# A two-layer trunk on one core: the front made token tile by token tile, the next quarter's rows in fewer steps, and one store on another queue

## The chip, the cores and the metric

The kernel runs on one core of a Trainium2 chip. The core has five engines, each with its own queue of instructions, which it takes in order: TensorE (PE in the profile; matmuls, its weight loads are PEld), VectorE (DVE), ScalarE (ACT), GpSimd (POOL) and SyncE (SP). SP computes nothing here; it issues DMA transfers between DRAM and the on-chip memory. The metric is the device time of one execution in microseconds (us).

## The reference, cut to what matters

The input is x, 2048 tokens of 1024 channels in float32, and a conditioning vector c of 1024. One layer of gMLP type is followed by one layer of attention type; both work on a normed and modulated x:

```python
def ada_mod(c, w, b, n):
    h = jax.nn.silu(c) @ w + b
    return jnp.split(h[:, None, :], n, axis=-1)

def gmlp_layer(x, c, ada_w, ada_b, norm_g, w_in, sgu_g, w_s, b_s, w_out):
    shift, scale, gate = ada_mod(c, ada_w, ada_b, 3)
    h = rms_norm(x, norm_g) * (1 + scale) + shift
    u, v, z = jnp.split(h @ w_in, 3, axis=-1)
    u = jax.nn.gelu(u)
    v = rms_norm(jax.nn.gelu(v), sgu_g)
    ...
    return x + gate * (y @ w_out)

def dilated_layer(x, c, kv_groups, ada_w, ada_b, norm_g, w_in, q_norm_g, w_out):
    shift, scale, gate = ada_mod(c, ada_w, ada_b, 3)
    h = rms_norm(x, norm_g) * (1 + scale) + shift
    qz = h @ w_in
    ...
    return x + gate * (y @ w_out)
```

Between the two, one set of keys and values for the attention is made from x after the first layer (w_kv). The widths that matter: u, v and z have 2048 columns each; the queries have three groups of 1024 columns and z of the second layer 1024.

## The kernel before

**Tiling.** The 2048 tokens are worked in four quarters Q of 512 tokens, each of four token tiles t of 128. The 1024 channels are eight slices k of 128. Every product of activations and weights is made of three matmuls (mm3, L214): both sides are split into a high part, rounded to the PE's faster float32 form, and the low rest, and high x high, high x low and low x high are added up in PSUM. So each weight tile of 128x512 is loaded into a tile "raw", copied by ACT into its high half (L187) and subtracted by DVE into its low half (L188) before PE can use it. hA (hAh and hAl) is the split, normed and modulated x of a quarter, transposed: channels on partitions, tokens along the row.

**The stages.** `begin` makes hA for the first quarter and the first two of four column blocks (j = 0, 1) of its v. Then for each quarter `layer_A` makes the rest of v, the mixing, u, z and the output product, adds it to x (the tiles xr, `done`), stores the sum x1d for the last stage, and norms it; `proj_B` makes from it keys and values (kv blocks), and queries and z of the second layer in blocks of 512x512 (q_block(2), kv, q_block(1), q_block(0), z_block). These last blocks (`dense_s`, and `dense_s2` for v of the later quarters) save an eighth of the products by working with sums of blocks: seven products of 24 matmuls each, on operands such as "s2" and weights such as wt, sums of blocks that were made once and stored in DRAM. m in the later quarters holds such sums of parts of hA.

**The front.** `begin` squares the eight slices of x (already transposed by the host) on ACT, adds them up over the channels with matmuls of one column (pssq), takes the power -1/2 on POOL (L816), and broadcasts the result over partitions with a matmul on a diagonal (prb). Meanwhile silu(c) is spread over all partitions (scb), and DVE makes scale and shift of each slice k as dots of scb with rows of the weights a_ada (aw; L152). The first slice of hA is made on DVE and ACT straight from prb (z0); slices 2 to 7 are multiplied with rb, a copy of prb, by POOL (L865). The products run slice by slice: for each k two column blocks j, four tiles t, three matmuls, 24 in all. `busy` puts transposes into PE's queue that compute nothing.

**Fillers.** Side work is written as Python generators. `tick` is called after the matmuls of each slice and lets the generators go on, by a share `rate` of a step each time; `drain` runs what is left to its end. `make_hA` is such a generator: during q_block(1), q_block(0) and z_block of one quarter, with rate 0.9, it prepares hA of the next. It loads x by rows, squares them on ACT, takes the reciprocal norms r on POOL, stores r to DRAM (rd, L710: 128x4 numbers, each a piece of 4 bytes), reads it back spread over all partitions (rb, L175), multiplies the transposed x (xT) with it, and for each k scales (h_a), splits (hAh by ACT, hAl by POOL) and stores h_a to DRAM (hd, L723), from which the parts of m are loaded (L743) for the sums. A `yield` in it is a stop; there are 27.

**What sets the order.** The build puts each engine's instructions into one fixed order, near that in which the code is written. Nearly all DMA transfers are issued by SP, one after the other, so one that waits for its data holds back all behind it. They run on 16 DMA engines, and SP waits, before it issues one, until the one eight places ahead of it has landed. Transfers land in about the order of their issue.

## Time and profile before

| | us |
|---|---|
| three executions | 2979.52, 2973.64, 2977.4 |
| median | 2977.4 |
| the profiled execution | 2983.25 |
| its span (first to last instruction) | 2981.5 |
| PE busy | 2889.6 |
| DVE, ACT, POOL busy | 2140.4, 1659.8, 772.2 |

The mean clock granted to PE is 0.988 of full speed; DMA moves 720.6 MB, 242 GB/s on average. PE is busy in 97% of the span, so the questions are where its holes lie and what ended them. In rows of a timeline the columns are start, duration, engine, line, operation, out<-in, shape and count, and in brackets how long the engine stood idle before it and what released it; numbers of tiles are left out of the names. In rows of SP the duration is that of issuing, not of the transfer.

### The profile page before, as it was taken

To read this page: it belongs to the slowest core of one execution; us is meant where nothing else is said; L and a number is where in the kernel's file an instruction comes from. 1 tells how busy PE (TensorE), PEld (TensorE's weight loads), DVE (VectorE), ACT (ScalarE), POOL (GpSimd) and SP (SyncE) were. 2 spreads that over 40 slices of the span, in tenths; PEclk is the share of its full clock that TensorE was granted. 3 is DMA by queue.
4 is the path that set the end of the run, shared out by engine and by line. 5 is a ranking of instruction groups with operands and counts; after the bars stand their busy time and mean duration, and the time that the engine had idled before them with its cause. 6 is when DMAs were issued, how large, how long until landed. Compare 5 with 4: busy or idle time off the path is not lost.

```text
span 2981.5 us, 45378 instructions
## 1 busy us (share of the span) xinstructions
PE 2889.6 (97%) x14519; PEld 2434.3 (82%) x14519; DVE 2140.4 (72%) x3997; ACT 1659.8 (56%) x3403; POOL 772.2 (26%) x1042
## 2 busy tenths in 40 slices
PE   8999999899999999899999999899999999999999
PEld 7788877787888878778888878778888888888887
DVE  6787467677777886767767876777759676877782
ACT  4433344567676355566655365676646366876541
POOL 2047432230000413510233403401314111122312
PEclk9999999999999999999999999999999999999999
DMA  6899977896789976787545977874335966788753
GB/s 230 276 333 340 308 259 212 254 306 216 252 302 306 347 237 218 244 283 241 179 131 165 343 236 231 260 262 142 107 111 182 361 214 219 246 265 323 241 176 110
DMA packets 389730, 720.60 MB, mean 242 GB/s; under 512 B 45426, under 2 KB 141810, under 8 KB 389492
## 3 DMA queue, kind: packets, MB, share of 16 engines
q1 hardware_dynamic: 389492, 717.71, 72.4%
q8 instruction: 115, 1.88, 0.3%
q14 instruction: 123, 1.01, 0.1%
HBM read 559.60 MB, written 157.96 MB: 241 GB/s over the span
## 4 chain that ended last, share of the span: by engine, by line
PE 63%; DMA 5%; DVE 3%; issue 3%; ACT 2%; POOL 1%; SPq 0%; POOLq 0%; DVEq 0%; ACTq 0%
PE pd_kv L216 6%; PE po L1314 4%; PE pd_z L260 3%; PE pd_z L258 3%; PE pd_z L259 3%; PE pd_u L260 3%; PE pd_u L258 3%; PE pd_u L259 3%; PE pd_o3a L216 1%; PE pd_o1a L216 1%; PE pd_o2a L216 1%; PE pm L900 1%; PE pd_v3b L216 1%; PE pq L1204 1%; PE pf L1498 1%
## 5 line engine op out<-in xcount | busy, mean ns | idle before, releaser
L216 PE MATMUL pd_kv<-w_kv,hkh 128*128 128x512 f32 x672 | 210.0, 393 | 2.8 <-DVE w_kv L188 2.3
L258 PE MATMUL pd_u<-hAh,w_u 128*128 128x512 f32 x512 | 206.4, 403 | 0.0
L258 PE MATMUL pd_z<-hAh,w_z 128*128 128x512 f32 x512 | 204.2, 399 | 0.0
L260 PE MATMUL pd_u<-hAh,w_u 128*128 128x512 f32 x512 | 200.5, 392 | 2.9 <-DVE w_u L188 2.9
L260 PE MATMUL pd_z<-hAh,w_z 128*128 128x512 f32 x512 | 200.0, 391 | 0.0
L259 PE MATMUL pd_u<-hAl,w_u 128*128 128x512 f32 x512 | 199.5, 390 | 0.0
L259 PE MATMUL pd_z<-hAl,w_z 128*128 128x512 f32 x512 | 199.4, 389 | 0.0
L1314 PEld LDWEIGHTS po<-kv,pT 128*128 128x128 f32 x1200 | 148.0, 191 | 11.0 <-ACT pT L1160 2.8
L1314 PE MATMUL po<-kv,pT 128*128 128x128 f32 x1200 | 150.6, 275 | 3.3 <-ACT pT L1160 2.3
L187 ACT ACTIVATE w_u<-raw_u 128x512 fp32r<-128x512 f32 x128 | 79.6, 629 | 132.9 <-DMA raw_u<-in_a_w_in_dram 54.2
L187 ACT ACTIVATE w_z<-raw_z 128x512 fp32r<-128x512 f32 x128 | 78.7, 628 | 129.6 <-PE pd_z L260 64.9
L216 PEld LDWEIGHTS pd_kv<-w_kv,hkh 128*128 128x128 f32 x672 | 125.9, 189 | 30.5 <-DVE w_kv L188 3.9
L1262 POOL TENSOR_TENSOR dg<-pr,ident 128x256 f32<-128x256 f32 x38 | 31.7, 833 | 424.8 <-DMA st_o<-od 226.6
L188 DVE TENSOR_TENSOR w_z<-raw_z,w_z 128x512 fp32r<-128x512 f32 x128 | 102.2, 806 | 53.5 <-ACT w_z L187 53.1
L216 PE MATMUL pd_kv<-w_kv,hkl 128*128 128x512 f32 x336 | 131.1, 391 | 0.0
L1085 POOL TENSOR_SCALAR s_q<-s_q 128x4 f32<-128x4 f32 x96 | 24.8, 258 | 386.7 <-DVE s_q L1084 288.1
L1254 ACT ACTIVATE pr<-pr,stat,rt 128x256 f32<-128x256 f32 (+1 forms) x192 | 104.1, 544 | 34.2 <-DVE stat L1248 19.9
L187 ACT ACTIVATE w_q<-raw_q 128x512 fp32r<-128x512 f32 x144 | 88.9, 627 | 52.7 <-DMA raw_q<-in_b_w_in_dram 17.8
L260 PEld LDWEIGHTS pd_u<-hAh,w_u 128*128 128x128 f32 x512 | 96.1, 188 | 24.6 <-DVE w_u L188 3.7
L188 DVE TENSOR_TENSOR w_q<-raw_q,w_q 128x512 fp32r<-128x512 f32 x144 | 96.7, 694 | 24.4 <-ACT w_q L187 23.4
L260 PEld LDWEIGHTS pd_z<-hAh,w_z 128*128 128x128 f32 x512 | 96.1, 188 | 20.8
L259 PEld LDWEIGHTS pd_z<-hAl,w_z 128*128 128x128 f32 x512 | 96.3, 188 | 18.1
(881 smaller groups left out, 8577.4 us busy)
## 6 DMA issues: line engine op xcount, KB each, us to landing
raw_q<-in_b_w_in_dram SPq DMA_DIRECT2D x144, 256.0 KB, 3.8
w_o<-wtd SPq DMA_DIRECT2D x72, 512.0 KB, 5.3
raw_u<-in_a_w_in_dram SPq DMA_DIRECT2D x128, 256.0 KB, 4.1
raw_z<-in_a_w_in_dram SPq DMA_DIRECT2D x128, 256.0 KB, 3.6
wtd<-cs SPq DMA_DIRECT2D x56, 512.0 KB, 3.9
raw_v<-in_a_w_in_dram SPq DMA_DIRECT2D x104, 256.0 KB, 4.0
qt<-qd SPq DMA_DIRECT2D x96, 260.0 KB, 3.3
od<-ot SPq DMA_DIRECT2D x96, 256.0 KB, 3.3
```

The costliest lines, as they stand in the source:

```text
L187: nc.scalar.activation(hi, src, AF.Copy)
L188: nc.vector.tensor_tensor(lo, src, hi.bitcast(F32), ALU.subtract)
L216: last_mm[0] = nc.tensor.matmul(pt, a, u[:, w, :], start=f, stop=e, skip_group_check=more)
L258: nc.tensor.matmul(pts[i], wh, hh[:, k, :], start=k == 0, stop=False)
L259: nc.tensor.matmul(pts[i], wh, hl[:, k, :], start=False, stop=False)
L260: nc.tensor.matmul(pts[i], wl, hh[:, k, :], start=False, stop=k == KT - 1)
L900: nc.tensor.matmul(pm[:, t * P:(t + 1) * P], m[e // 8][:, t, (e % 8) * P:(e % 8 + 1) * P], wst[:, e // 2, :], start=True, stop=True)
L1204: nc.tensor.transpose(pq[:, h * P:(h + 1) * P], u["qt"][:, h * P:(h + 1) * P], ident)
L1254: nc.scalar.activation(pr[:, i, :], pr[:, i, :], AF.Exp, bias=mneg[:, i:i + 1], scale=u["rt"][:, h:h + 1], accum_out=lsum[:, i:i + 1])
L1262: nc.gpsimd.tensor_tensor(dg, prev, ident.unsqueeze(1).broadcast_to([P, hp, P]), ALU.mult)
L1314: nc.tensor.matmul(po[:, h * P:(h + 1) * P], u["pT"][h // hp][:, h % hp, j, :], u["kv"][:, j, kh, 1, :], start=j == 0, stop=j == nk - 1)
L1498: nc.tensor.matmul(pt, yb[:, 0, k, :], w_[:, 0, :], start=k == 0, stop=False)
```

## The change

**1. The front.** x of the first quarter comes from the host by token tiles (xt0), each one transfer of 128 partitions x 8 slices x 128 tokens (512 KB, in pieces of 512 bytes on chip). Each tile is squared (`square`), normed, broadcast and scaled (`rows`) by itself, POOL multiplying slices 2 to 7 of one tile at a time, and the products of k=0 run tile by tile behind it; from k=1 on they run slice by slice as before, with the two column blocks of a tile next to each other. The ada rows of k=0 are loaded first, then c, then x. Fillers on PE stand between the steps. **2. make_hA**: two tiles are squared in one step, the loads of xT and the store of r share a step, and each k has one stop instead of two: 16 in all. **3.** The store of x1d of the first quarter (where `fast` is false) is issued by ACT instead of SP.

In the hunk of `begin`, "..." stands for the removed lines (L774 to L867 above).

```diff
@@ -695,7 +695,8 @@
         yield
         sq = sp.tile([P, 16], F32, tag="sqa", bufs=1, name=f"sqa{Q}")
         for t in range(TPQ):
-            yield
+            if t == 2:
+                yield
             for h in range(2):
                 j = evt(f"sqj{Q}{t}{h}")
                 nc.scalar.activation(j, xts[t][:, h * 512:(h + 1) * 512], AF.Square,
@@ -705,18 +706,17 @@
         r = rstd_of(sq[:, 8:12], TPQ, D, f"r_a{Q}")
         zs = [xp.tile([P, 2, QT], F32, tag="xin", name=f"xT{Q}_{k2}") for k2 in range(0, KT, 2)]
         for i, z in enumerate(zs):
-            nc.sync.dma_start(z, xt[Q, :, 2 * i:2 * i + 2, :])
-        yield
+            nc.sync.dma_start(z, xt[Q - 1, :, 2 * i:2 * i + 2, :])
         nc.sync.dma_start(rd[Q].rearrange("t p -> p t"), r[:, 0:TPQ])
         yield
         yield
         rb = bcast(rd[Q:Q + 1].rearrange("o t p -> o (t p)"), f"rb{Q}")
         yield
         yield
+        yield
         for k in range(KT):
             z = zs[k // 2][:, k % 2, :]
             nc.vector.tensor_tensor(z, z, rb, ALU.mult)
-            yield
             h = evt(f"h_a{Q}_{k}")
             nc.scalar.activation(h, z, AF.Identity, scale=aff[0][:, k:k + 1], bias=aff[1][:, k:k + 1])
             nc.scalar.activation(hA[0][:, k, :], h, AF.Copy)
@@ -771,107 +771,139 @@
         xT = big.tile([P, KT, QT], F32, tag="big", name="xT0")
         one = rp.tile([P, 512], F32, tag="raw", name="one")[:, 0:P]
         nc.vector.memset(one, 1.0)
...
+        crow = wp.tile([P, D], F32, tag="w", name="crow")[0:1, :]
+        aws, raws, us = {}, {}, {}
+        def load_aw(k, i):
+            if k % 2 == 0 and k not in aws:
+                t = big.tile([P, 2, 2, D], F32, tag="big", name=f"aw{k}")
+                aws[k], aws[k + 1] = t[:, 0], t[:, 1]
+            nc.sync.dma_start(aws[k][:, i, :], a_ada[i * KT + k])
+        def load_w(k):
+            for j in range(2):
+                raws[k, j] = rp.tile([P, 512], F32, tag="raw", name=f"raw_v0{j}_{k}")
+                nc.sync.dma_start(raws[k, j], a_w_in[k * P:(k + 1) * P, AW + j * 512:AW + (j + 1) * 512])
+        def w_high(k, j):
+            us[k, j] = wp.tile([P, 2, 512], F32R, tag="w", name=f"w_v0{j}_{k}")
+            nc.scalar.activation(us[k, j][:, 0, :], raws[k, j], AF.Copy)
+        def w_low(k, j):
+            nc.vector.tensor_tensor(us[k, j][:, 1, :], raws[k, j], us[k, j][:, 0, :].bitcast(F32), ALU.subtract)
+        def load_xt(t):
+            nc.sync.dma_start(xT[:, :, t * P:(t + 1) * P], xt0[t])
+        load_aw(0, 1)
+        nc.sync.dma_start(crow, c)
+        load_aw(0, 0)
+        nc.sync.dma_start(vecs, cols)
+        load_xt(0)
+        load_xt(1)
+        load_w(0)
+        load_xt(2)
+        load_xt(3)
+        def dots(k, i):
+            ks = slice(k, k + 1)
+            ada_dot(aff[1 - i][:, ks], aws[k][:, i, :], aab_c[:, i * KT + k:i * KT + k + 1])
+            if i:
+                nc.vector.scalar_tensor_tensor(aff[0][:, ks], aff[0][:, ks], 1.0, ang_c[:, ks],
+                                               ALU.add, ALU.mult)
+        pq = pst("pq0")
+        prb = pst("prb", "d")
 
         def busy(n):
...
             for _ in range(n):
...
+                nc.tensor.transpose(pq[:, 256:384], ident, ident)
         r = sp.tile([P, 16], F32, tag="sqa", bufs=1, name="sqa0")
...
+        rb, diag, z0, h0 = (evt(f"{n}0") for n in ("rb", "diag", "z", "h"))
+        def square(t):
+            j = wp.tile([P, KT, P], F32, tag="w", name=f"sqT{t}")
+            nc.scalar.activation(j, xT[:, :, t * P:(t + 1) * P], AF.Square)
+            for k in range(KT):
+                nc.tensor.matmul(pq[:, t:t + 1], j[:, k, :], one[:, 0:1], start=k == 0, stop=k == KT - 1)
+            nc.vector.tensor_scalar(r[:, t:t + 1], pq[:, t:t + 1], 1.0 / D, EPS, ALU.mult, ALU.add)
+            nc.gpsimd.tensor_tensor(r[:, t:t + 1], r[:, t:t + 1], mhalf[:, 0:1], ALU.pow)
+        def rows(t):
             sl = slice(t * P, (t + 1) * P)
             nc.scalar.activation(diag[:, sl], ident, AF.Copy, scale=r[:, t:t + 1])
             nc.tensor.matmul(prb[:, sl], one, diag[:, sl], start=True, stop=True)
...
+            nc.vector.tensor_tensor(z0[:, sl], xT[:, 0, sl], prb[:, sl], ALU.mult)
+            nc.scalar.activation(hA[0][:, 0, sl], z0[:, sl], AF.Identity, scale=aff[0][:, 0:1],
+                                 bias=aff[1][:, 0:1])
+            nc.vector.tensor_scalar(h0[:, sl], z0[:, sl], aff[0][:, 0:1], aff[1][:, 0:1], ALU.mult, ALU.add)
+            nc.vector.tensor_tensor(hA[1][:, 0, sl], h0[:, sl], hA[0][:, 0, sl].bitcast(F32), ALU.subtract)
+            nc.scalar.activation(rb[:, sl], prb[:, sl], AF.Copy)
+            nc.gpsimd.tensor_tensor(xT[:, 2:KT, sl], xT[:, 2:KT, sl],
+                                    rb[:, sl].unsqueeze(1).broadcast_to([P, KT - 2, P]), ALU.mult)
+        pts = {}
+        def products(k, t):
+            sl = slice(t * P, (t + 1) * P)
+            for j in range(2):
+                if k == 0:
+                    pts[j, t] = pst(f"pd_v0{j}_{t}", "da"[j])
+                mm3(pts[j, t], hA[0][:, k, sl], hA[1][:, k, sl], (us[k, j]), k == 0, k == KT - 1)
+        busy(4)
+        for n in range(2):
+            pc = pst(f"pc{n}")
+            nc.tensor.matmul(pc, one[0:1, :], crow[:, n * 512:(n + 1) * 512], start=True, stop=True)
+            nc.scalar.activation(scb[:, n * 512:(n + 1) * 512], pc, AF.Silu)
+        busy(30)
+        dots(0, 1)
+        dots(0, 0)
+        square(0)
+        busy(6)
+        square(1)
+        w_high(0, 0)
+        rows(0)
+        w_low(0, 0)
+        w_high(0, 1)
+        w_low(0, 1)
+        busy(4)
+        for t in range(TPQ):
+            products(0, t)
+            if t + 2 < TPQ:
+                square(t + 2)
+            busy(4)
+            if t == 2:
+                for i in (1, 0):
+                    load_aw(1, i)
+                load_w(1)
+                dots(1, 1)
+            if t + 1 < TPQ:
+                rows(t + 1)
+        for k in range(1, KT):
             h = xT[:, k, :]
             if k == 1:
+                dots(1, 0)
                 nc.vector.tensor_tensor(h, h, rb, ALU.mult)
...
+            nc.scalar.activation(h, h, AF.Identity, scale=aff[0][:, k:k + 1], bias=aff[1][:, k:k + 1])
+            split(hA[0][:, k, :], hA[1][:, k, :], h)
+            for j in range(2):
+                w_high(k, j)
+                w_low(k, j)
             if k + 1 < KT:
...
+                for i in (1, 0):
+                    load_aw(k + 1, i)
+                load_w(k + 1)
+                dots(k + 1, 1)
+                dots(k + 1, 0)
+            for t in range(TPQ):
+                products(k, t)
         m, sqv = v_tiles(0)
         for j in range(2):
             ev = v_evac(0, m, sqv, j)
             for t in range(TPQ):
...
+                ev(t, pts[j, t])
         return hA, m, sqv
 
     def layer_A(Q, hA, m, sqv, j0):
@@ -971,7 +1003,7 @@
             if seen[t] == 2:
                 tt = Q * TPQ + t
                 def store():
-                    nc.sync.dma_start(x1d[tt * P:(tt + 1) * P, :], xts[t])
+                    (nc.sync if fast else nc.scalar).dma_start(x1d[tt * P:(tt + 1) * P, :], xts[t])
                 if fast:
                     stores.append([0, store])
                 else:
@@ -1567,7 +1599,8 @@
                                      "a_sgu_g", "k_norm_g", "b_q_norm_g")]
     return {
         "x": x,
-        "xt": np.ascontiguousarray(x[0].reshape(NQ, QT, KT, P).transpose(0, 3, 2, 1)),
+        "xt0": np.ascontiguousarray(x[0, :QT].reshape(TPQ, P, KT, P).transpose(0, 3, 2, 1)),
+        "xt": np.ascontiguousarray(x[0, QT:].reshape(NQ - 1, QT, KT, P).transpose(0, 3, 2, 1)),
         "c": np.asarray(i["c"]),
         "cols": np.ascontiguousarray(np.concatenate(cols, axis=1)),
         "a_ada": _tiles(np.asarray(i["a_ada_w"])[0]),
```

How this moves instructions, at three places. First DVE in the front; affa 180 and 181 are scale and shift, sqa takes the sums of squares, w_v is a weight's low half. Before, from the last sum of squares on:

```order
L815 TENSOR_SCALAR sqa_290<-pssq_213 128x1
L152 ISA aw_315,affa_180<-aw_315,scb,vecs 128x1024
L152 ISA affa_180 128x1
L829 SCALAR_TENSOR_TENSOR affa_180<-affa_180,vecs 128x1
L842 TENSOR_TENSOR z_331<-xT_188,prb 128x512
L152 ISA aw_315,affa_181<-aw_315,scb,vecs 128x1024
L152 ISA affa_181 128x1
L856 TENSOR_TENSOR xT_188<-xT_188,rb_338 128x512
L843 TENSOR_SCALAR xT_188<-z_331,affa_180,affa_181 128x512
L846 TENSOR_TENSOR w_v_0_322<-raw_v_0_321,w_v_0_322 128x512
L847 TENSOR_TENSOR hAl_187<-xT_188,hAh_186 128x512
L848 TENSOR_TENSOR w_v_0_326<-raw_v_0_325,w_v_0_326 128x512
```

Now:

```order
L152 ISA aw_192,affa_180<-aw_192,scb,vecs 128x1024
L152 ISA affa_180 128x1
L152 ISA aw_192,affa_181<-aw_192,scb,vecs 128x1024
L152 ISA affa_181 128x1
L812 SCALAR_TENSOR_TENSOR affa_180<-affa_180,vecs 128x1
L793 TENSOR_TENSOR w_v_0_285<-raw_v_0_199,w_v_0_285 128x512
L830 TENSOR_SCALAR sqa_207<-pq_205 128x1
L793 TENSOR_TENSOR w_v_0_296<-raw_v_0_201,w_v_0_296 128x512
L152 ISA aw_192,affa_180<-aw_192,scb,vecs 128x1024
L152 ISA affa_180 128x1
L830 TENSOR_SCALAR sqa_207<-pq_205 128x1
L837 TENSOR_TENSOR z_210<-xT_188,prb 128x128
```

The dots of k=0 stand ahead of the first norm now, and operations on a single tile (128x128) alternate with weight halves and dots of k=1, so each of these can hold the tile behind it.

Second, SP in q_block(1) and the product after it, for the first quarter; wt_1, wt_0 and wt_3 name the weights of three products. Before:

```order
L195 DMA raw_q00t_0_5105<-wt_1_108 128x512
L195 DMA raw_q00t_1_5110<-wt_1_108 128x512
L708 DMA xT_6_5014<-in_xt_dram 128x1024
L710 DMA rd<-r_a_5008 128x4x1
L195 DMA raw_q00t_2_5115<-wt_1_108 128x512
L195 DMA raw_q00t_3_5120<-wt_1_108 128x512
L195 DMA raw_q_0_5151<-in_b_w_in_dram 128x512
L175 DMA rb_5184<-rd 128x512
L195 DMA raw_q_1_5156<-in_b_w_in_dram 128x512
```

Now:

```order
L1123 DMA qd_94<-st_q02w_4348 128x520
L1123 DMA qd_94<-st_q02w_4349 128x520
L709 DMA xT_2_4848<-in_xt_dram 128x1024
L709 DMA xT_4_4849<-in_xt_dram 128x1024
L709 DMA xT_6_4850<-in_xt_dram 128x1024
L710 DMA rd<-r_a_4844 128x4x1
L195 DMA raw_q01t_0_4867<-wt_0_111 128x512
L195 DMA raw_q01t_1_4872<-wt_0_111 128x512
L195 DMA raw_q01t_2_4877<-wt_0_111 128x512
L195 DMA raw_q01t_3_4882<-wt_0_111 128x512
L1123 DMA qd_94<-st_q02u_4067 128x520
L1123 DMA qd_94<-st_q02u_4068 128x520
```

The store of r (rd) stood between the weight tiles of wt_1; now it stands, right behind the loads of xT, ahead of those of wt_0, which are used four products earlier.

Third, SP at the end of the z block; raw_v and raw_v14t are weights of the next quarter's v. Before:

```order
L723 DMA hd<-h_a_5_5851 128x2x256
L723 DMA hd<-h_a_6_5857 128x2x256
L723 DMA hd<-h_a_7_5863 128x2x256
L195 DMA raw_v_0_6039<-in_a_w_in_dram 128x512
L195 DMA raw_v_1_6044<-in_a_w_in_dram 128x512
L195 DMA raw_v_2_6049<-in_a_w_in_dram 128x512
L743 DMA m_1_5872<-hd 128x1024 x2
L195 DMA raw_v_3_6054<-in_a_w_in_dram 128x512
L195 DMA raw_v14t_0_6089<-wt_1_124 128x512
```

Now the last two stores of h_a:

```order
L195 DMA raw_z0bt_0_5665<-wt_2_121 128x512
L195 DMA raw_z0bt_1_5670<-wt_2_121 128x512
L723 DMA hd<-h_a_6_5533 128x2x256
L723 DMA hd<-h_a_7_5587 128x2x256
L1207 DMA kv_2_7181<-kvd 128x512
```

and, some twenty rows further on, the loads of m:

```order
L195 DMA raw_z0b_2_5833<-in_b_w_in_dram 128x512
L195 DMA raw_z0b_3_5838<-in_b_w_in_dram 128x512
L743 DMA m_1_5878<-hd 128x1024 x4
L1131 DMA zd<-zb_2_5762 128x512
L1131 DMA zd<-zb_3_5765 128x512
L195 DMA raw_v_0_5891<-in_a_w_in_dram 128x512
```

The stores of h_a stood among the weights of v, with two of the loads of m behind them; now the last of them is among the weights of the z block (raw_z0bt), and all four loads of m stand ahead of the first raw_v.

More of the change, by code (lines that the diff above doesn't have):

```diff
@@ L791, in units @@
-        def units(k):
-            us[k] = [wunits(a_w_in, k, AW + j * 512, f"v0{j}_{k}_", 1)[0] for j in range(2)]
+        crow = wp.tile([P, D], F32, tag="w", name="crow")[0:1, :]
[9 more added lines that the diff above has]
+                nc.sync.dma_start(raws[k, j], a_w_in[k * P:(k + 1) * P, AW + j * 512:AW + (j + 1) * 512])
@@ L796, in busy @@
             for _ in range(n):
-                nc.tensor.transpose(pw[:, 0:P], ident, ident)
-        for n in range(2):
-            pc = pst(f"pc{n}")
-            nc.tensor.matmul(pc, one[0:1, :], crow[n], start=True, stop=True)
-            nc.scalar.activation(scb[:, n * 512:(n + 1) * 512], pc, AF.Silu)
-        pqs = [pst(f"pssq{t}", "d") for t in range(TPQ)]
-        sqs = [evt(f"sqT{k}") for k in range(4)] + [rp.tile([P, 512], F32, tag="raw", name=f"sqT{k}")
-                                                    for k in range(4, KT)]
@@ L806, in begin @@
-        for k in range(KT):
-            nc.scalar.activation(sqs[k], xT[:, k, :], AF.Square)
-            for t in range(TPQ):
-                nc.tensor.matmul(pqs[t][:, 0:1], sqs[k][:, t * P:(t + 1) * P], one[:, 0:1],
-                                 start=k == 0, stop=k == KT - 1)
-            if k + 1 < KT:
-                busy(3)
-        r = sp.tile([P, 16], F32, tag="sqa", bufs=1, name="sqa0")
-        for t in range(TPQ):
-            nc.vector.tensor_scalar(r[:, t:t + 1], pqs[t][:, 0:1], 1.0 / D, EPS, ALU.mult, ALU.add)
```

64 lines of the change are left out of this document (1 added, 63 removed).

## Prediction

> **What bounds the kernel now.** I read the busy table first, then what TensorE (PE) waited for, then the timelines around each long wait. A row of the waits reads: who waited, for which engine's tile; us in all, times, longest.
>
> ```profile
> PE 2889.6 (97%) x14519; PEld 2434.3 (82%) x14519; DVE 2140.4 (72%) x3997; ACT 1659.8 (56%) x3403; POOL 772.2 (26%) x1042
> ...
> PE pd_q00b L216 <- DVE st_q01u L511: 8.9, 1, 8.9
> PE pd_q20b L216 <- DVE st_q21u L511: 7.9, 1, 7.9
> PE pd_q10b L216 <- DVE st_q11u L511: 7.4, 1, 7.4
> PE pt_b L637 <- DVE xr L984: 6.8, 2, 6.4
> PE pd_v1a L216 <- ACT w_v14t L187: 4.3, 1, 4.3
> PE pd_v2b L216 <- ACT w_v L187: 3.3, 1, 3.3
> PE pd_v3b L216 <- ACT w_v L187: 3.1, 1, 3.1
> ...
> PE pd_v2b L216 <- ACT hAh L722: 2.1, 1, 2.1
> ...
> PE pd_v3b L216 <- ACT hAh L722: 1.3, 1, 1.3
> ```
>
> PE is the bound: 2889.6 of 2981.5 us, so only 92 us of holes are there to be won, and the change adds or removes almost no matmul time. The rows name three families, each of which comes once for each of the later quarters: the q products (24.2 us), the start of the v products of the next quarter (14.1 us), and one wait of 6.4 at the end of the first quarter. A fourth place is the front, before PE streams at all:
>
> ```profile
> 33.00 0.73 PE L216 MATMUL pd_v<-w_v,hAh 128*128 128x512 f32 x2 [1.28 <-ACT hAh L844]
> ...
> 46.17 2.11 PE L216 MATMUL pd_v<-w_v,hAh 128*128 128x512 f32 x8 [0.59 <-ACT hAh L187]
> ```
>
> The first real product runs at 33.0 us, and k=1 starts at 46.17, after which no row of the timeline has a wait until the last product of the front. So the front is worth exactly what moves the start of k=1: seven steps of 24 matmuls follow, whatever came before.
>
> **The front.** Removed: a norm over all 512 tokens before anything is multiplied. In its place come 4 tiles of 128 tokens, each with its own square, power, broadcast and scaling, and fillers on PE which cost nothing as long as PE has only holes there. What sets the first step is the first tile's x and the silu behind it:
>
> ```profile
> 4.29 0.63 ACT L807 ACTIVATE sqT<-xT 128x512 f32<-128x512 f32 x1 [2.23 <-DMA xT<-in_xt_dram]
> 4.94 1.28 ACT L802 ACT_TABLE_LOAD   x1
> 6.23 1.09 ACT L802 ACTIVATE scb<-pc 128x512 f32<-128x512 f32 x2
> ...
> 11.94 0.63 ACT L807 ACTIVATE sqT<-xT 128x512 f32<-128x512 f32 x1 [0.29 <-DMA xT<-in_xt_dram]
> 24.80 2.06 POOL L816 TENSOR_TENSOR sqa<-sqa,mhalf 128x4 f32<-128x4 f32 x1 [21.27 <-DVE sqa L815]
> 26.89 1.28 ACT L822 ACTIVATE diag<-ident,sqa 128x128 f32<-128x128 f32 x4 [14.32 <-POOL sqa L816]
> ```
>
> Eight slabs of 256 KB came between 4.29 and 11.94, 1.09 us each. The first tile (512 KB) now stands behind two ada pieces of 512 KB: six slabs, so 4.29 + 5 x 1.09 = 9.7 us. ACT then does in order a square of twice the width (1.1, estimated from 0.63), a table load 1.28, a silu 0.55, the second tile's square 1.1, a silu 0.55: 14.3. DVE's order has both dots of k=0 ahead of the first norm (1.28 each), and one weight low half: 17.7. The power takes 2.06: 19.8. From the power to the first broadcast matmul 0.5 us, then quarter-width z and hAh, some 1 us: the first product at about 21.3 instead of 33.0.
>
> But k=1 comes only when DVE is through. By its order, from the first norm to the multiplication for k=1 it does 5 dots, 6 low halves, 12 operations of quarter width and that multiplication. What these take depends on POOL:
>
> ```profile
> 31.29 9.75 POOL L865 TENSOR_TENSOR xT<-xT,rb 128x512 f32<-128x512 f32 x6 [4.43 <-ACT rb L850]
> 34.78 1.74 DVE L846 TENSOR_TENSOR w_v<-raw_v,w_v 128x512 fp32r<-128x512 f32 x1
> 42.05 1.27 DVE L152 CUSTOM_DVE_ANT_0 aw<-aw,scb,vecs 128x1024 f32<-128x1024 f32 x1
> 44.64 0.82 ACT L858 ACTIVATE xT<-xT,affa,affa 128x512 f32<-128x512 f32 x1 [10.65 <-DVE affa L829]
> 47.12 0.69 DVE L188 TENSOR_TENSOR hAl<-xT,hAh 128x512 fp32r<-128x512 f32 x1
> ```
>
> A subtraction of this width took 1.74 while POOL multiplied and 0.69 after: a factor of 2.5. Undisturbed, 5 x 1.28 + 6 x 0.65 + 12 x 0.25 (estimated from 0.69 for four times the width) + 0.69 + 0.5 = 14.5 us, from 17.7 to 32.2. POOL's work is unchanged in elements, four bursts of 9.75/4 = 2.44 us, all now inside this stretch: they cost DVE 9.75 x (1 - 1/2.5) = 5.9: 38.1. ACT's scaling 0.82 and high half 0.63 follow: k=1 at about 39.5, 6.7 us before 46.17. I take **7**. Upper bound: no disturbance, 33.6, a gain of 12.6. Lower: POOL's whole 9.75 added to DVE and 5 us more for dots that wait in DVE's row for the later ada pieces, which no row prices: 48.4, a loss of 2.
>
> The Trainium skill (SBUF — State Buffer, "SBUF: two separate sides") says that DVE and GpSimd hold their shared port pair as an exclusive lock, the later one blocked for the whole instruction. The rows agree so far (1.74 against 9.75/6 = 1.63 for one POOL operation), and by the rule POOL's 9.75 us would be added whole: 3.9 us less gain than I take. The sum goes by the rows' factor.
>
> **Scaled rows in fewer steps.** For each later quarter a filler squares x, writes the reciprocal norms r to DRAM (rd, L710), reads them back as a broadcast (rb) and makes hA. It has 27 stops before and 16 after, and the three product blocks it runs in step it 3 blocks x 7 products x 4 x 0.2857 x 0.9 = about 21.6 times, so now it can end inside them. What the r store does to the queue is the cause of the 8-us stalls:
>
> ```profile
> 560.40 0.33 SPq L708 DMA_DIRECT2D xT<-in_xt_dram  x1
> 565.35 0.37 SPq L710 DMA_DIRECT2D rd<-r_a  x1
> 565.81 0.93 SPq L195 DMA_DIRECT2D raw_q00t<-wt  x2
> 578.33 0.63 ACT L187 ACTIVATE w_q00t<-raw_q00t 128x512 fp32r<-128x512 f32 x1 [13.21 <-DMA raw_q00t<-wt]
> 1868.29 12.01 DMA raw_q20t<-wt
> 1882.50 7.94 PE L216 MATMUL pd_q20b<-w_q20t,hob 128*128 128x512 f32 x24 [7.93 <-DVE st_q21u L511]
> ```
>
> The waits name DVE L511, but ACT's row names the true one: weights issued right behind the r store land 12 us after issue (565.81 to 578.33; 12.01 in the third quarter's chain of waits), since the store's 512 pieces of 4 bytes go ahead of them. Before that SP itself stood for 5 us, until r was ready. After such a stall 24 matmuls took 7.94, elsewhere 5.60: some 2 us more. So one quarter loses 24.2/3 + 2 = 10.1.
>
> The store stays as it is, but stands four products earlier (wt_0, wt_3 and two of w_q lie between): ahead of the raw_q01t of wt_0, whose product PE ran from 549.60 on.
>
> ```profile
> 529.05 0.62 ACT L701 ACTIVATE sqj<-x 128x512 f32<-128x512 f32 x1
> 535.62 2.42 SPq L195 DMA_DIRECT2D raw_q01t<-wt  x4
> ...
> 549.60 5.60 PE L216 MATMUL pd_q01b<-w_q01t,hob 128*128 128x512 f32 x24
> ```
>
> With squares from 529 on in two steps a product (5.6) apart, 4 squares of 0.8 with their sums and POOL's power, the store is issued at about 538.5. The four weight pieces behind it, issued so far from 535.6, come at 539 + 12.4 = 551.4, and 1.3 us go to their halves: 552.7 against 549.6. So the stall is smaller, not gone: 3.1 at least; I take 4.5 plus 1.5 for the restart, 6 instead of 10.1, three times: **12** won. Bounds: nothing won (the full 12 us again, with SP standing), or the whole 30 (the transfers further ahead cover it).
>
> **The next quarter's v.** With the old 27 stops the remainder ran in one piece at the end of the z block:
>
> ```profile
> 658.66 2.81 SPq L723 DMA_DIRECT2D hd<-h_a  x3
> 664.40 0.80 SPq L743 DMA_DIRECT2D m<-hd  x2
> 659.94 4.24 POOL L725 TENSOR_TENSOR hAl<-h_a,hAh 128x512 fp32r<-128x512 f32 x3 [4.42 <-ACT hAh L722]
> 683.12 6.33 PE pd_v1a L216 x22
> ```
>
> The last row is from the chain of waits. hd stores at 658.66, the loads of m from them at 664.4, then DVE's sums and their high halves, and only behind these, on ACT, the weight half (w_v14t in the first fence) for which PE stood 4.3 us. In the new order all eight hd stores stand in the middle of the z block, and the four m loads together, ahead of the first raw_v. The waits 4.3 + 3.3 + 3.1 + 2.1 + 1.3 = 14.1 should go with their cause, and 1.3 us of slow restart each (22 matmuls in 6.33, against 5.60 x 22/24 = 5.1): 18 in all. The four m loads, 2 MB in one block ahead of the weights, take some of it back; I take two thirds, **12**, bounds 6 and 18. The POOL and DVE work of the eight k steps moves into the q and z blocks, where PE's rows hide it now only if DVE has room (a rival below).
>
> **x1d by ACT.** The wait of 6.4 at the first quarter's end is xr scaled in place, which must wait until its store has read it:
>
> ```profile
> 402.82 0.86 SPq L974 DMA_DIRECT2D x1d<-xr  x2
> 403.35 0.61 ACT L969 ACTIVATE xo<-xr 128x512 f32<-128x512 f32 x1
> ```
>
> SP issued both stores from 402.82, before ACT's square. In ACT's new order each store stands behind its tile's square, hence at about 404, a microsecond later; in return the weights behind it on SP go sooner. **0**, bounds -2 and +1.
>
> **Sum.** 7 + 12 + 12 + 0 = 31: from the profiled execution's own 2983.25 (1.75 more than its span) to 2952. That execution lies 5.9 above the median of the runs, 2977.4; against the median I forecast 2947.
>
> **Rivals.** (a) *The r store's 12 us are only moved.* For it: the store has the same 512 pieces, and SP waits in front of it for POOL as before. Against: the pieces before it in the queue are further ahead. Then the second term is 0: 2977.4 - 19 = 2958. (b) *The front gains nothing*, because DVE's row, with four POOL bursts in it, ends at 46 anyway: 2954. (c) *All holes close*: front 12.6, 30 and 18: 61, 2916. (d) *Slower: the rows' work crowds DVE.* The eight k steps a quarter now run beside products whose weights DVE must halve; POOL's hAl takes 4.24/3 = 1.4 us, slows DVE's 0.69 to 1.74, and each of the 24 steps delays a product by one such operation and its restart, 1.5 us: 36 us lost, with the q stalls staying whole and 19 won elsewhere: +17, 2994. It decides where DVE has under 2 us to spare in a product of 5.6; over the span it is busy 72%, 4.0 of 5.6, so one delayed operation should fit: that speaks against it. (e) *An earlier front is eaten later*: the transfers set the pace.
>
> ```profile
> 160.00:280.00 120.00, 120.00 (x579) 101.16 (x578) 99.74 (x105) 41.36 (x68) 75.69 (x49) 1.00 1.01 340
> ```
>
> From 160 to 280 us the DMA share is 1.01, with PE nevertheless busy all 120 us; if the transfers set that pace, the 7 us go: 2954, as in (b).
>
> **How the numbers follow.** The forecast gets 0.50, (a) 0.15, (b) and (e) 0.12, (c) 0.08, (d) 0.09, and 0.06 is left for small gains and losses that cancel. What can be told from no change is 0.2%, 6 us. Faster is the forecast, (a), (b), (e), (c): 0.85; same 0.06; slower (d): 0.09. The range: at the low end the front at its upper bound and half of what the other two leave, 19 more than the forecast: 2928; at the high end only 8 us of the boundary: 2970.
>
> **What would show it.** Front: first product near 21, k=1 near 40. The q stalls: st_q?1u waits of 7 to 9 gone, waits of 3 to 6 at the product of wt_0 (st_q?1, four products earlier), and the weights behind the r store still landing 12 us after issue. The boundary: no wait of pd_v?a or pd_v?b above 2 us. The forecast is wrong if k=1 starts after 45, if the q waits still sum to 24, or if new waits of DVE low halves (L188) stand in the q and z blocks.

## The result, and the profile after

The changed kernel takes 2950.91 us (median of four executions, 2950.17 to 2954.5), the kernel before 2975.75 (2973.64 to 2979.52, the three shown above and one beside the changed kernel): a ratio of 0.9918, interval 0.9900 to 0.9935, 24.8 us less. Run again later, it gave 0.9921 (0.9908 to 0.9933). The forecast was 2947 in a range of 2928 to 2970, with 30 us less. The time lies near it, but the parts do not: one term had the wrong sign, and two others were larger than I took them, so that the sum came out close is in part luck. One of the four executions of e5 below took 12503 us, for a reason that no run here shows; its median in the table counts all four, its ratio the other three.

The table of PE's waits after, as it was read before; the rows of pd_v are the front and its v, those of pd_q?1b the q products, those of pd_v1a and pd_v2a the next quarter's v:

```profile
PE 2883.6 (98%) x14534; PEld 2430.2 (82%) x14534; DVE 2150.4 (73%) x4006; ACT 1659.6 (56%) x3405; POOL 772.3 (26%) x1043
...
PE pd_v L216 <- DVE hAl L841: 6.0, 3, 2.5
PE pd_q01b L216 <- ACT w_q01t L187: 4.2, 1, 4.2
PE pd_v2a L216 <- ACT w_v L187: 4.2, 1, 4.2
PE pd_q11b L216 <- ACT w_q11t L187: 3.9, 1, 3.9
PE pd_v L216 <- DVE w_v L188: 3.5, 1, 3.5
PE pt_b L637 <- DVE xr L1016: 3.4, 3, 1.8
PE pd_v1a L216 <- ACT w_v L187: 2.7, 1, 2.7
...
PE pd_q21b L216 <- ACT w_q21t L187: 2.3, 1, 2.3
```

The q waits have gone from 24.2 to 10.4 us, the longest ones of the v products from 4.3, 3.3 and 3.1 to 4.2 and 2.7. Where PE stands at some points of the program, in us from the start of the profiled execution (one of each kernel):

| point on PE | before | after | difference |
|---|---|---|---|
| first product of the front | 33.0 | 24.9 | -8.1 |
| k=1 of the front | 46.2 | 44.8 | -1.4 |
| end of the first quarter's v | 128.1 | 135.0 | +6.9 |
| first output product | 320.6 | 325.0 | +4.3 |
| first q product, quarter 0 | 464.5 | 464.7 | +0.2 |
| first z product, quarter 0 | 614.6 | 609.6 | -5.0 |
| end of v, quarter 1 | 738.4 | 729.8 | -8.7 |
| first z product, quarter 1 | 1258.5 | 1243.9 | -14.6 |
| end of v, quarter 2 | 1384.1 | 1367.6 | -16.4 |
| first z product, quarter 2 | 1917.5 | 1897.2 | -20.3 |
| end of v, quarter 3 | 2043.1 | 2012.9 | -30.2 |
| last product | 2976.4 | 2947.4 | -29.0 |

So PE was ahead for a moment in the front, lost it again before 135 us, was even at the end of the first quarter, and won at each q block and each start of v. Here is the front, from PE's timeline:

```profile
24.87 2.05 PE L216 MATMUL pd_v<-w_v,hAh 128*128 128x512 f32 x4
...
33.29 0.74 PE L216 MATMUL pd_v<-w_v,hAl 128*128 128x512 f32 x2 [1.42 <-DVE hAl L841]
...
39.13 0.73 PE L216 MATMUL pd_v<-w_v,hAl 128*128 128x512 f32 x2 [2.50 <-DVE hAl L841]
...
43.09 0.73 PE L216 MATMUL pd_v<-w_v,hAl 128*128 128x512 f32 x2 [2.04 <-DVE hAl L841]
44.79 2.93 PE L216 MATMUL pd_v<-w_v,hAh 128*128 128x512 f32 x6 [0.98 <-ACT hAh L187]
...
110.26 0.79 PE L216 MATMUL pd_v<-w_v,hAh 128*128 128x512 f32 x1 [3.49 <-DVE w_v L188]
...
113.83 1.05 PE L216 MATMUL pd_v<-w_v,hAh 128*128 128x512 f32 x2
```

There are three losses in it. Each tile's low half comes late from DVE. At 44.79 PE runs slowly: six matmuls of k=1 in 2.93 us, and its 24 matmuls take until 51.98, 7.2 us at a granted clock of 0.76, where k=1 before took 5.6 at 1.00. In the traces of the other runs with this front (the changed kernel run again, e1, e5, e6 and e7, all explained below) it took 7.0 to 7.4 us; with the old front 5.6 in e3, e4 and e8, but 7.2 in e2. And at 110 us there is a wait that the kernel before does not have, again with slow matmuls behind it (clock 0.50 from 110.3 to 116.4): from 106.4 to 118.5 PE did what takes 5.44 us elsewhere, 6.7 us lost. The 1.4 us that k=1 came earlier, 1.6 us for k=1 itself and these 6.7 make the 6.9 of the table.

### The profile page after: what moved, and what is told of

It reads as the page before. It is cut to its first block, busy times and chain, and to the rows that moved or that the text cites. A ratio compares the mean times of both kernels' runs of the same rounds, so it can differ in the third digit from the quotient of the medians.

```text
span 2952.7 us, 45415 instructions
## 1 busy us (share of the span) xinstructions
PE 2883.6 (98%) x14534; PEld 2430.2 (82%) x14534; DVE 2150.4 (73%) x4006; ACT 1659.6 (56%) x3405; POOL 772.3 (26%) x1043
## 4 chain that ended last, share of the span: by engine, by line
PE 71%; DMA 11%; DVE 7%; issue 4%; ACT 4%; POOL 2%; SPq 1%; POOLq 0%; DVEq 0%; ACTq 0%
PE pd_kv L216 6%; PE pd_z L258 4%; PE pd_z L260 4%; PE pd_z L259 4%; PE po L1346 4%; PE pd_u L258 4%; PE pd_u L260 4%; PE pd_u L259 4%; PE pm L932 2%; PE pd_o2a L216 1%; PE pd_v2a L216 1%; PE pd_o1a L216 1%; PE pd_v1a L216 1%; PE pd_v1b L216 1%; PE pd_o L216 1%
## 5 line engine op out<-in xcount | busy, mean ns | idle before, releaser
L1346 PEld LDWEIGHTS po<-kv,pT 128*128 128x128 f32 x1200 | 148.1, 191 | 10.4 <-ACT pT L1192 2.2
L181 POOL TENSOR_SCALAR rv<-sqv 128x1 f32<-128x1 f32 x16 | 7.3, 458 | 408.1 <-DVE sqv L922 407.7
```

Source lines behind the costliest of these rows:

```text
L181: nc.gpsimd.tensor_scalar(t[:, 0:n], ssq, 1.0 / width, EPS, ALU.mult, ALU.add)
L1346: nc.tensor.matmul(po[:, h * P:(h + 1) * P], u["pT"][h // hp][:, h % hp, j, :], u["kv"][:, j, kh, 1, :], start=j == 0, stop=j == nk - 1)
```

## The experiments

All ratios are against the kernel before, run on the same chip.

### Each part alone

```diff
 # e1: the new begin and xt0, with make_hA and the x1d store of before
 # e2: make_hA of the change, with begin and the x1d store of before
 # e3: only this line
-                    nc.sync.dma_start(x1d[tt * P:(tt + 1) * P, :], xts[t])
+                    (nc.sync if fast else nc.scalar).dma_start(x1d[tt * P:(tt + 1) * P, :], xts[t])
 # e4: e2 and e3 together, the change without its front
```

> Before with the new front alone (old scaled rows, x1d stored by SP). In the changed kernel PE starts k=1 at 44.8 instead of 46.2 us, but the products of the front's v end 6.9 us later, the loss coming at 107 to 118 us behind the store of gd. Theory A: the delay is in the front itself, but the wait at the end of the first quarter (6.4 us, set by transfers) takes it up: time within -1 to +3 us of before. Rival B: the delay stays to the end, and the changed kernel only hides it by the store on ACT: +4 to +7 us. Rival C, the prediction: 7 us less than before.

> Before with the scaled rows in 16 steps alone (old front, x1d stored by SP). From the stages of the two traces, the q products gained 15.6 us and the next quarter's v products about 15. Theory A: -25 to -31 us, all that the changed kernel has gained. The prediction: -24. Rival: under -20, part of the gain belongs to the front or the store.

> Before with the first quarter's x1d stored by ACT alone. Theory A: ACT cannot issue before its own weight copy, which waits for raw_kv until 402.7 us, so the store leaves when SP issued it too: within 2 us of before, and the wait of PE at 409 still 5 us or more. Rival B: -4 to -6 us, the wait of 6.4 us shrinks to 2.

> The changed kernel with the old front put back (new rows, store by ACT). Theory A: front and store are each worth nothing in the end, so the same as the changed kernel within 3 us, about 2948 to 2952. Rival B: the front costs 4 to 7 us and the store wins them back, so 2944 to 2947. Rival C (the prediction): 7 us slower than the changed kernel.

| version | median us | ratio | interval | difference, us |
|---|---|---|---|---|
| e1, front alone | 2972.40 | 1.0013 | 1.0002 to 1.0024 | +3.9 |
| e2, rows alone | 2942.82 | 0.9912 | 0.9898 to 0.9925 | -26 |
| e3, store alone | 2967.22 | 0.9989 | 0.9980 to 0.9999 | -3 |
| e4, rows and store | 2940.93 | 0.9906 | 0.9892 to 0.9920 | -28 |

(The difference is the ratio times the 2970.2 us of before there.) The parts add up: 3.9 - 26 - 3 = -25, and the changed kernel has -24.8. The rows carry the whole gain, as theory A had it; the interval, 22 to 30 us, holds the prediction's 24 too. e4 lies some 4 us below the changed kernel by the ratios (0.9906 and 0.9918), inside the intervals; its 2940.93 us are under what theories A and B had for it, and rival C, 7 us slower, is excluded.

The front alone is slower by 0.6 to 7 us; my 7 us gain is excluded. Its interval leaves open whether that is theory A's 0 to 3 or rival B's 4 to 7. Its trace shows the course of the changed kernel: v ends 5.6 us late, and the lag shrinks from 5.5 us at the first output product to 0.8 at the first q product. What takes it up is the wait at the end of the first quarter, 2.28 us instead of 6.44:

```profile
410.38 0.63 PE L637 MATMUL pt_b<-ident,xr 128*128 128x128 f32 x4 [2.28 <-DVE xr L1016]
```

For the store, e3's interval reaches from almost nothing (-0.3) to -6. In four traces (before, changed, e3, e4) the first instruction in ACT's row before the stores is a weight copy that waits for raw_kv; of the store alone:

```profile
399.63 0.63 ACT L187 ACTIVATE w_kv<-raw_kv 128x512 fp32r<-128x512 f32 x1 [13.23 <-DMA raw_kv<-in_w_kv_dram]
399.71 0.83 ACTq L974 DMA_DIRECT2D x1d<-xr  x2
```

and of e4:

```profile
402.75 0.63 ACT L187 ACTIVATE w_kv<-raw_kv 128x512 fp32r<-128x512 f32 x1 [12.67 <-DMA raw_kv<-in_w_kv_dram]
402.83 0.82 ACTq L974 DMA_DIRECT2D x1d<-xr  x2
```

In e4 ACT issues at 402.83, no earlier than SP did (402.82), as theory A said; in e3 raw_kv came 3 us earlier, and the wait of PE is 2.5 us instead of 6.4. A's other sign, that this wait stays at 5 us or more, fails in both: it is 4.2 in e4. Whether moving the store made raw_kv come earlier there, or that execution, stays open. From rows alone to rows and store the step is 1.9 us, inside both intervals.

### What the small stores cost

In the changed kernel two transfers stand ahead of late weights. One is r (rd, L710), which I had named. The other I had not looked at: gd (L171), the gate of the first layer, 128x8 numbers, 1024 pieces of 4 bytes. The same line of `ada_gate` also stores the gate of the second layer (gc_gb), at 473 us in the changed kernel, so an edit of it changes two stores. Both kinds were written as rows instead: transposed on PE, copied by DVE and stored in pieces of 512 bytes.

```diff
 # e5, in make_hA
-        nc.sync.dma_start(rd[Q].rearrange("t p -> p t"), r[:, 0:TPQ])
         yield
+        pr_ = pst(f"prr{Q}")
+        nc.tensor.transpose(pr_[0:TPQ, 0:P], r[:, 0:TPQ], ident)
+        rr = evt(f"rr{Q}")[0:TPQ, 0:P]
+        nc.vector.tensor_copy(rr, pr_[0:TPQ, 0:P])
+        nc.sync.dma_start(rd[Q], rr)
 # e6, in ada_gate (both gates): the same for col[:, 0:KT] and gd, 8 rows
 # e8: both in the version with the old front (e4); e7: both in the changed kernel
```

> The changed kernel again, as the measure for the runs beside it. 0.990 to 0.9935 of before, as it was. The sum of its parts run alone (front +4, rows -26, store -3) gives -25 us, 0.9914.

> The changed kernel with r of the later quarters transposed on PE (128x4 to 4x128) and stored as 4 rows of 512 bytes instead of 512 pieces of 4. If the pieces make the transfers behind the store late (the prediction's cause): the store and the weights behind it land within 4 to 6 us of issue instead of 13, PE's waits for w_q?1t (4.2, 3.9, 2.3 and some 2 us of slow restart each) go, 10 to 15 us less than the changed kernel. Rival: the queue is only full, whatever the store's pieces: the weights still take 10 us or more, and the time stays within 4 us.

> The changed kernel with the gate's column (gd, 128x8, 1024 pieces of 4 bytes) transposed on PE and stored as 8 rows of 512 bytes; the store then also stands behind the last weights of v. If the front's loss is this store ahead of four weight tiles: no wait at 107 to 118 us, the front's v ends 6 to 7 us earlier, at about 128; of that 2 to 7 us reach the end, the rest goes into the longer wait at the first quarter's end. Rival: the wait at 110 us stays, since the ada loads queue there in any case; the same time.

> The old front, the new scaled rows, the store by ACT, and both small stores written as rows. If both causes hold: the 0.9906 of the version with the old front less 10 to 15 us, 0.985 to 0.988. Rival: the same as that version, 0.99.

| version | median us | ratio | interval |
|---|---|---|---|
| the changed kernel again | 2946.58 | 0.9921 | 0.9908 to 0.9933 |
| e5, r as rows | 2931.31 | 0.9868 | 0.9850 to 0.9887 |
| e6, gd as rows | 2938.41 | 0.9889 | 0.9876 to 0.9903 |
| e8, both, old front | 2923.26 | 0.9840 | 0.9826 to 0.9853 |

Both theories held, at or just above the upper end of what they had: 15.3 us for r, 8.2 for gd. e8 lies just below its 0.985 to 0.988. The store of r in the changed kernel, then the row of ACT that waits behind it and PE's:

```profile
538.43 0.38 SPq L710 DMA_DIRECT2D rd<-r_a  x1
539.06 2.41 SPq L195 DMA_DIRECT2D raw_q01t<-wt  x4
...
549.06 5.74 SPq L195 DMA_DIRECT2D raw_q01t<-wt  x4
552.49 2.33 ACT L187 ACTIVATE w_q01t<-raw_q01t 128x512 fp32r<-128x512 f32 x4 [7.17 <-DMA raw_q01t<-wt]
553.17 7.60 PE L216 MATMUL pd_q01b<-w_q01t,hob 128*128 128x512 f32 x24 [4.23 <-ACT w_q01t L187]
```

and with r as rows (e5), SP, ACT and PE:

```profile
536.74 2.21 SPq L709 DMA_DIRECT2D xT<-in_xt_dram  x3
539.67 2.47 SPq L195 DMA_DIRECT2D raw_q01t<-wt  x4
...
554.30 0.27 SPq L715 DMA_DIRECT2D rd<-rr  x1
554.67 1.30 SPq L195 DMA_DIRECT2D raw_q<-in_b_w_in_dram  x3
555.95 1.27 ACT L187 ACTIVATE w_q<-raw_q 128x512 fp32r<-128x512 f32 x2 [0.65 <-DMA raw_q<-in_b_w_in_dram]
558.17 1.33 ACT L187 ACTIVATE w_q<-raw_q 128x512 fp32r<-128x512 f32 x2
550.30 2.88 PE L216 MATMUL pd_q01b<-w_q01t,hob 128*128 128x512 f32 x12
553.02 0.27 PE L712 MATMUL prr<-ident,r_a 128*4 128x128 f32 x1
553.04 3.01 PE L216 MATMUL pd_q01b<-w_q01t,hob 128*128 128x512 f32 x12
```

The weights right behind the store land 13.4 us after issue in the one (539.06 to 552.4), 3.2 in the other (554.67 to 557.9), and PE goes through with one transposition of 0.27 us between. But the two stores do not stand in the same place: in the changed kernel three loads of xT (1.5 MB) are issued just ahead of it, in e5 it comes 16 us later, among weights. The fair comparison is that of the same weights, raw_q01t, right behind the same loads: they land 7.2 us after issue in e5 (539.67 to 546.84), where no store stands between. So, by one execution of each, some 6 of the 13.4 us are the store's, and the rest is the queue's without it. The table of e5's waits has no row of w_q any more. The other four q weights of the changed kernel show how the queue passes it on: SP issued the next four only from 549.06.

For gd, in the front: in the changed kernel SP issues:

```profile
89.23 0.38 SPq L171 DMA_DIRECT2D gd<-gc_ga  x1
...
91.50 2.72 SPq L195 DMA_DIRECT2D raw_v<-in_a_w_in_dram  x2
94.26 13.09 SPq L158 DMA_DIRECT2D aw_ksh<-in_kv_ada_dram  x4
110.23 0.93 SPq L195 DMA_DIRECT2D raw_v<-in_a_w_in_dram  x2
```

In the kernel before only two tiles of v's weights stood behind gd, here four, the last two at 110.2. In e6 the store of gd comes later too, at 115.38, behind the last weights of v. What it does to the transfers shows in the ten microseconds behind it, in the columns us, then busy us of PE, PEld, DVE, ACT and POOL, the clock, the DMA share and GB/s; the changed kernel, then e6, each with the stretch of PE's wait as a second row:

```profile
90.00:100.00 10.00, 10.00 (x45) 8.28 (x45) 1.29 (x2) 5.17 (x13) 0.00 (x0) 1.00 0.68 33
107.00:118.00 11.00, 7.74 (x21) 6.13 (x22) 9.70 (x17) 4.08 (x9) 0.00 (x0) 0.69 0.89 310
```

```profile
115.40:125.40 10.00, 10.00 (x45) 8.26 (x44) 5.54 (x9) 3.69 (x8) 0.00 (x0) 1.00 0.93 333
107.00:118.00 11.00, 11.00 (x51) 9.01 (x50) 9.72 (x17) 4.50 (x10) 0.00 (x0) 1.00 0.84 291
```

For ten microseconds the DMA engines are busy to 68% and move 33 GB/s, against 333 behind the store as rows. Since e6 changes the store's form and its place, it does not tell which of the two took PE's wait away. In e6 PE's wait at 110 is gone (another of 1.25 us stands at 97), but v ends at 132.6, not at 128, since in that execution k=1 itself came at 47.2. So the trace places some 5 of e6's 8.2 us, the 6.7 lost at 110 less the new wait; the rest is within the intervals. Part of it is probably the second gate's: in the changed kernel the weights right behind its store (raw_q02t, issued at 473.88) land after 10.4 us, ACT waits for them, and PE stands 1.6 us for ACT in that block (pd_q02a); in e6, where that store too comes later and as rows, these weights land 3.5 to 5.5 us after issue and the wait is gone.

### What holds up the new front

```diff
 # e9: in rows(t), POOL's multiplication is taken out, and after the loop over t:
+        for k in range(2, KT):
+            nc.gpsimd.tensor_tensor(xT[:, k, :], xT[:, k, :], rb, ALU.mult)
 # e10: square(1), square(2), square(3) ahead of the first product
 # e11: both; all three on top of e7
```

> The changed kernel (new front) with both small stores written as rows. If the new front by itself, freed of the gd store, is worth nothing against the old one: 0.984 of before, as the version with the old front and both stores as rows. If it still costs: 0.985 to 0.987. The prediction (k=1 earlier by 7 us): 0.982. In the trace k=1 starts between 44.8 and 47.7 us as in the other versions with the new front.

> The version with both stores as rows, and POOL multiplies slices 2 to 7 only once all four tiles have been normed (six operations of 128x512, as the old front has it). In the changed front three DVE operations of one tile took 1.83 to 1.91 instead of 0.3 us, each to the end of the POOL operation beside it. If that holds DVE up, these take 0.3 and k=1 starts 4 to 5 us earlier than in the version beside it. Rival: DVE waits for PE's squares in any case, and k=1 comes within 1 us of it. In time: 0 to 4 us less.

> The version with both stores as rows, and the squares of all four tiles ahead of the first product. In the changed front DVE stood 6 us in all (2.1, 2.2, 2.1) for the sums of squares that PE made behind other work. If this serial turn of PE, DVE, POOL, ACT and PE sets the front: k=1 starts 3 to 6 us earlier than in the version beside it, though the first product comes some 2 us later. Rival: POOL's bursts then come closer together and DVE loses as much to them: within 1 us.

> Both: squares first and POOL's multiplication late. If the two delays add up: k=1 7 to 10 us earlier, at 37 to 40 us, which is what the prediction had, and up to 7 us less than the version beside it. Rival: what is won in the front is taken up by the wait at the end of the first quarter, 0 to 2 us less.

| version | median us | ratio | interval | k=1 at | k=2 at |
|---|---|---|---|---|---|
| e7, both as rows, new front | 2920.31 | 0.9830 | 0.9816 to 0.9843 | 48.8 | 56.0 |
| e9, POOL late | 2925.05 | 0.9845 | 0.9832 to 0.9859 | 46.2 | 58.9 |
| e10, squares first | 2920.46 | 0.9831 | 0.9818 to 0.9845 | 45.8 | 52.3 |
| e11, both | 2921.51 | 0.9836 | 0.9821 to 0.9851 | 41.1 | 51.9 |

(e8, the old front beside e7: 0.9840, k=1 at 46.0, k=2 at 51.6.) In DVE's and POOL's rows of the changed kernel the two delays can be seen:

```profile
20.36 0.16 DVE L830 TENSOR_SCALAR sqa<-pq 128x1 f32<-128x1 f32 x1 [2.13 <-PE pq L829]
25.05 0.16 DVE L830 TENSOR_SCALAR sqa<-pq 128x1 f32<-128x1 f32 x1 [2.24 <-PE pq L829]
29.76 0.16 DVE L830 TENSOR_SCALAR sqa<-pq 128x1 f32<-128x1 f32 x1 [2.08 <-PE pq L829]
31.33 1.91 DVE L841 TENSOR_TENSOR hAl<-h,hAh 128x128 fp32r<-128x128 f32 x1
40.40 1.83 DVE L840 TENSOR_SCALAR h<-z,affa,affa 128x128 f32<-128x128 f32 x1
30.94 2.15 POOL L843 TENSOR_TENSOR xT<-xT,rb 128x768 f32<-128x768 f32 x1
40.04 2.11 POOL L843 TENSOR_TENSOR xT<-xT,rb 128x768 f32<-128x768 f32 x1 [2.53 <-ACT rb L842]
```

DVE stands three times for sums of squares that PE makes in its own turn behind other work; and hAl, 0.28 us elsewhere, takes 1.91, until just after POOL's operation ends (30.94 + 2.15 = 33.09; 31.33 + 1.91 = 33.24). Neither e9 nor e10 took its delay away. In e9 POOL's six multiplications come in one block of 9.70 us from 40.43 on, in which h and hAl of the last tile and the multiplication for k=1 take 1.30, 1.35 and 1.77 us. In e10 DVE stands for the sums of squares no shorter, only earlier, 8.9 us in all against e7's 8.2, and then meets POOL four times instead of three, as the rival had it:

```profile
15.82 0.16 DVE L838 TENSOR_SCALAR sqa<-pq 128x1 f32<-128x1 f32 x1 [0.77 <-PE pq L837]
19.86 0.16 DVE L838 TENSOR_SCALAR sqa<-pq 128x1 f32<-128x1 f32 x1 [2.78 <-PE pq L837]
23.70 0.16 DVE L838 TENSOR_SCALAR sqa<-pq 128x1 f32<-128x1 f32 x1 [2.48 <-PE pq L837]
27.53 0.16 DVE L838 TENSOR_SCALAR sqa<-pq 128x1 f32<-128x1 f32 x1 [2.86 <-PE pq L837]
```

k=1 comes 2.6 and 3.0 us earlier than in e7 (4 to 5 and 3 to 6 expected), but that shows no gain: e7's 48.8, above the 44.8 to 47.7 that I expected, is the latest of six executions of the same front (44.8, 45.5, 47.2, 47.3, 47.7, 48.8). Counted from the first square of x, k=1 starts after 36.0 to 39.1 us in these six, after 37.2 in e9 and 37.7 in e10. Only both steps together lie outside: 32.9 us, 3 to 6 less. k=1 at 41.1 comes near the 39.5 that the prediction had. But the gain does not last: with POOL late, PE waits 2.6 (e9) and 2.7 us (e11) for DVE's low halves in the middle of k=1, and k=2 starts at 58.9 (e9) and 51.9 (e11), no earlier than in the old front. In time no difference between e7, e10, e11 and e8 is clear of the intervals. What e9 lost against e7, 0.15%, lies inside them too; 0 to 4 us less was expected. So the new front, freed of the gate's store, may be worth what the old one was (0.984 expected for e7 then) or a few us more: the prediction's 0.982 lies inside e7's interval as well.

e7 takes 2920.31 us, 51 less than the kernel before beside it (2971.19) and, by the ratios 0.9830 and 0.9921, some 27 less than the changed kernel, clear of the intervals of both.

## Why the prediction was right, and where it was wrong

**What bounds the kernel**: right. PE's waits named the places where the gain came; PE's busy time moved by 6 us, and the gains lie in stretches where PE had waits.

**The front, 7 us won: wrong in sign**, 4 us lost (0.6 to 7). x and the first norm came as worked out (the square at 8.75 for 9.7, the first sum of squares at 16.27 for 17.7). The step that failed is the next: "k=1 comes only when DVE is through", with 14.5 us of DVE's operations laid end to end. DVE's row also holds three sums of squares that wait for PE, 2.1 + 2.2 + 2.1 = 6.5 us, and PE's row had them behind the fillers and ahead of prb and of the first product (a square's matmuls took up to 3.4 us). The engines took turns for each tile, where I had priced one engine's work. From the first norm to the multiplication for k=1 (16.27 to 42.83) DVE's row took 26.6 us where the sum had 20.4: these 6.5, another 1.9 of waits for prb, 4.6 lost to POOL, and 13.7 of operations for the 14.5. This is read from one trace; e9 to e11 do not isolate its parts. The first product came at 24.9 instead of 21.3, k=1 at 44.8 instead of 39.5, and in other executions at 45.5 to 48.8, past the 45 that I had named as the sign of being wrong. Of POOL's disturbance, 5.9 in the sum, the trace has 4.6: 1.6, 1.5 and 1.5 us beyond the undisturbed 0.28 and 0.34.

Two things had no term. The 24 matmuls of k=1 took 7.2 us instead of 5.6, at the lower clock. PE had been busy for 4.2 of the 10 us ahead of them, and for 8.4 of 10 before. That the idle time is the cause is my reading, and the old front's 7.2 in e2 shows that it is not the new front's alone. And the new order of SP put gd ahead of four weight tiles, 6.7 us. I had gone through the order of SP only where the diff touched the program; the transfers that a filler issues at the same time moved against it.

The Trainium skill's rule (SBUF — State Buffer, "SBUF: two separate sides"), that of a DVE and a GpSimd instruction which both need their shared ports the later one is blocked for the other's whole length, fits the rows better than my factor of 2.5: hAl and h of 128x128 took 1.83 to 1.91 us, each ending within 0.2 us of POOL's operation, where the factor gives 0.7 to 0.9. The sum that I had worked out by it, POOL's 9.75 us added whole, was further off than mine, since DVE met POOL only three times.

**The rows, 12 us in the q blocks**: right in mechanism, short in size. The store of r was issued at 538.43 (538.5), the weights behind it landed at 552.4 (551.4), PE stood 4.2 us (4.5 taken), and in the two later quarters 3.9 and 2.3. From the first q to the first z product each quarter won 5.2 us, 15.6 in all. Against e5, where these waits are gone, the three stretches are 32.8 us longer in the kernel before (30.2 taken: the old stalls cost more behind them than the 2 us that I had for the restart) and 17.2 in the changed one (18 taken). That the 4-byte pieces make the transfers behind them late was an inference; e5 bears it out for some 6 of the 13.4 us; the rest is the queue behind the loads of xT, which stand right ahead of the store only in the new order and which I had not priced.

**The next quarter's v, 12 us**: from the end of z to the end of v the three quarters won 3.7, 3.2 and 9.9, 16.8 us. The remainder that I kept for the four m loads ahead of raw_v is there: PE waits 2.7 and 4.2 us for w_v at the start of two of them, though my sign was that no wait there exceeds 2. In the first, the last load of m lands at 645.3, DVE's sums and their copies on ACT follow until 648.9, and only behind these and two of zb does ACT copy w_v, at 649.9, whose first tile had landed at 647.2: the place of ACT's copy behind the sums, which I had named as the old cause, is still there. e2, with both row terms, has 22 to 30 us for my 24. Since it is one execution against one, the split between the two terms is less sure than their sum.

**x1d by ACT, 0**: -3 (-6 to 0), just outside the bounds (-2 to 1), which the interval overlaps. That ACT's store leaves no earlier than SP's is right in the changed kernel and in e4 (402.97 and 402.83 against 402.82).

**The rivals.** (a) fell, though part of its stall stayed: 10.4 of 24.2 us. (b) was nearest to what the front did, for a reason of its own, and (e), that a later place eats it, holds at another place than I named: the wait at the first quarter's end took up some 4 us of the front's loss in e1, and it takes up a lead as well: e8's old front ends v 5.6 us ahead of e7's new one, and 1.1 us are left behind that wait (3.2 us in e8, 0.3 in e7). The stretch that I had named for it, 160 to 280 us, did nothing of the kind. (c) fell with the front. (d) fell: the only new wait of PE for a weight's low half in the q and z blocks is 0.2 us long. The sum came out 6 us too good: 11 us too much for the front, against some 2 too little for the rows and 3 for the store, each by the times of the part alone: without the rows' and the store's surplus the front's miss would have nearly doubled the error. The low end of the range was said to lie 19 us under the forecast; its parts as I named them add up to 5.6 + 12 = 17.6.

## What to carry to other kernels

When work is cut into pieces that pass through four engines, price one piece's whole round with the waits of each in-order row, not one engine's work end to end. And look at what the new order puts ahead of the loads: a store of a few KB that falls into pieces of 4 bytes held the queue for some 6 to 10 us, and turning five such stores into rows on TensorE, 0.3 us for one of r, was worth as much as the change itself.

## What was not expected of the hardware

A store of 2 KB in 512 pieces of 4 bytes landed 9.7 us after issue in the kernel before (the second quarter's) and 13.8 in the changed one behind three loads of 512 KB; one of 4 KB in 1024 pieces took 11.0. The weights issued right behind a store landed only after it, and during the larger one the DMA engines were 68% busy at 33 GB/s. DVE operations of 0.3 us took 1.8 to 1.9 when they came behind a POOL operation of 2.1.
